# Context norms as late steps, the first norm's factor applied late, and shift columns made in the filler

## The chip, the cores and the metric

One core of one Trainium2 chip. TensorE (PE) multiplies matrices; its weight loads are listed as PEld. VectorE is DVE, ScalarE is ACT, GpSimd is POOL, and SyncE (SP) issues the transfers. The metric is the device time of one execution in microseconds (us).

## The reference

Two models, one after the other, on `x` of 512 tokens by 1024 features, all in float32.

The first has two layers. Each layer is: a gated feed-forward block (SwiGLU, inner width 2816), a mixer (sparse attention beside a gated MLP), and a second feed-forward block. Each of the three starts with an RMS norm whose scale and shift come from a vector `c` through a large matrix (`ada_w`): `n = rms(h) * g * (1 + scale) + shift`. The first model ends with `rms(h) * final_g`.

The second model has two layers on `x` (512 tokens) and on a context `ctx` (256 tokens). Layer 0 mixes tokens by mean pooling over windows of 2, 4, 8 and 16 positions, one window size for each quarter of the features, and then by a 256x256 matrix for each quarter; layer 1 by attention. After each mixer comes an MLP with squared ReLU (inner width 4096). All norms are modulated in the same way. Layer 0 runs on the context too, and layer 1 reads its result:

```
y = pool_mixer(modulate(rms_norm(x, g_mix_pre), sh1, sc1))
x = x + gt1 * rms_norm(y, g_mix_post)
m = sq_relu_mlp(modulate(rms_norm(x, g_mlp_pre), sh2, sc2))
x = x + gt2 * rms_norm(m, g_mlp_post)
```

## The kernel before

**Layout and products.** The residual `h` is kept transposed, features on partitions, as eight chunks of 128x512. Every float32 factor is split into a rounded part and a remainder (`hi`, `lo`), and a product is three matmuls (`mm3`, lines 114 to 116). A weight tile is loaded to one of three `raw` buffers (`wload`), copied to `whi` by ACT (line 98), and its remainder `wlo` is made by DVE or POOL (line 100). `psum()` takes one of six banks `mm`; two more banks, `aux`, take small products.

**Order of the queues.** The program is written as Python that traces instructions. A planner then orders each engine's queue: trace order is the priority, and its own estimates of durations decide what it takes to be ready. Where an instruction's input is later than estimated, the engine stands before it.

**Norms.** `Rms.add` squares a chunk on ACT and adds it into `ssum` on DVE or POOL (line 150). `mean` multiplies `ssum` by ones on PE (line 163), `rsqrt` takes eleven small DVE instructions (lines 128 to 133), `bcast` spreads the factor over the partitions by four PE transposes (line 202). `RmsPE` (line 181 and 183) multiplies each squared chunk by ones on PE instead and sums in PSUM; it is used once, for the pooled `y`.

**First tiles of a block.** `Pre` lets PE start on a block's first four weight tiles before the norm is known. The tail of the block before calls `Pre.chunk` for each new chunk of `h`; `Pre.issue` then multiplies the weights by the unnormalised chunks and applies the factor afterwards (`take`, line 377). The part of the product that comes from the shift is one column for each tile: `Pre.shift` multiplies the raw tile by the shift on POOL and sums it (lines 269, 274, 276), `column` finishes it by a product with ones (line 288), `bias` copies the four columns to `shb` (line 341). All this lies in the block's beginning, where DVE and PE also work on the norm.

**Filler.** Each feed-forward block (`ffn`) runs side work between its products: `run_steps(filler, nf[0])` after each pair of input tiles and `nf[1]` after each two output tiles. It consists of the products with `ada_w` (`ada_steps`, line 399, tiles `adaw` in three buffers), and in the last block, `ffn(1, 1)`, also of `ctx_steps`: the context's norm, `pool_mix`, the norm of its result, the residual and the next norm. In `pool_mix` each quarter `g` does two chunks of pooling on DVE and ACT and then at once its two products; the three norms are each one step.

**The pool stage.** The tail of `ffn(1, 1)` is `FinalTail`: it keeps two sums of squares, and multiplies each chunk by the pooling matrices (`project`). Four tables (`band`) are loaded and copied by ACT at line 1183 before the last output tiles start. After the block comes the pool stage of `x`, with steps of the context's MLP (`ctx`, `mlp_steps`) put between by hand (`WEAVE`): first factors (`factors`, line 1218), rescaled tiles (`pooled`, line 1234), then for each of eight chunks a product with the band (`windows`, lines 1247 and 1251), a copy (1366), the corrected edges (1369), the sum of squares, and line 1371, which applies the first model's last norm to `h`. Then `ry.finish()`, the residual (`post`, lines 1077 and 1078) with `Pre.chunk`, the first MLP tiles (`issue_two`), and the normed chunks (`normed`, lines 218 and 224). The context's MLP has, for each of eight parts, four input steps of 24 matmuls and eight output steps of 12, all 256 wide.

Of the kernel before, what the change touches and what calls it, by code (L numbers as in the profile page):

```python
# [18 lines left out]
D = 1024  # L19
# [18 lines left out]
WEAVE = (1, 3, 4, 1.65, 1)  # L38
# [13 lines left out]
def build(tc, d, stop=99):  # L52
# [83 lines left out]
    class Rms:  # L136


        def __init__(self, N, tmp, tag=""):
            self.N, self.n, self.tmp = N, 0, tmp  # L140
            p = norm_p if N == S and not tag else cur["cx"]
            self.acc = p.tile([128, N], F32, name=f"ssum{N}{tag}", tag=f"ssum{N}{tag}")
# [16 lines left out]
        def mean_steps(self):  # L159
            nt = self.N // 128  # L160
            st = psum(aux, "aux")
            for j in range(nt):
                T.matmul(st[:, j:j + 1], self.acc[:, j * 128:(j + 1) * 128], ones[:, 0:1], start=True, stop=True)
                yield
            v = small.tile([128, nt], F32, name="rs_v", tag="rs_v")
            V.tensor_scalar(v, st[:, :nt], 1.0 / D, EPS, op0=OP.mult, op1=OP.add)
            yield v
# [3 lines left out]

    class RmsPE(Rms):


        def __init__(self, N, tmp):
            self.N, self.n, self.tmp = N, 0, tmp
            self.st = psum(aux, "aux")

        def add(self, src, scale=1.0, eng=None):
            sq = self.tmp("sq")[:, :self.N]  # L180
            A.activation(sq, src, AF.Square, scale=scale)
            for j in range(self.N // 128):
                T.matmul(self.st[:, j:j + 1], sq[:, j * 128:(j + 1) * 128], ones[:, 0:1],
                         start=self.n + j == 0, stop=self.n == DC - 1 and j == self.N // 128 - 1)
            self.n += 1

        def mean_steps(self):
            nt = self.N // 128
            v = small.tile([128, nt], F32, name="rs_v", tag="rs_v")
            V.tensor_scalar(v, self.st[:, :nt], 1.0 / D, EPS, op0=OP.mult, op1=OP.add)  # L190
            yield v
# [34 lines left out]

    class Pre:
# [3 lines left out]
        def __init__(self, gs, sh, tmp):  # L231
            self.gs, self.sh, self.tmp = gs, sh, tmp
            self.rms = Rms(S, tmp)
            self.hi, self.lo = [], []
            self.cols = psum(aux, "aux")
            self.pss = []
            self.scaled = {}

        def chunk(self, k, src):
            hi, lo = rtile(), rtile()  # L240
            A.activation(hi, src, AF.Copy, scale=self.gs[:, k:k + 1])  # L241
            V.scalar_tensor_tensor(lo, src, self.gs[:, k:k + 1], hi.bitcast(F32), op0=OP.mult, op1=OP.subtract)
            self.hi.append(hi)
            self.lo.append(lo)
            self.rms.add(src, eng=G if k < 4 else V)
# [17 lines left out]
        def shift(self, raw):  # L263

            u = [shp_p.tile([128, 256], F32, name="shp", tag="shp") for _ in range(2)]
            n = 2
            for e, k in enumerate((0, 2, 4, 6)):
                o = u[min(e, 1)]
                G.tensor_tensor(o.rearrange("p (k m) -> p k m", k=n),  # L269
                                raw[:, k * 128:(k + n) * 128].rearrange("p (k m) -> p k m", k=n),  # L270
                                self.sh[:, k:k + n].rearrange("p (k o) -> p k o", o=1).to_broadcast([128, n, 128]),
                                op=OP.mult)
                if e > 0:
                    G.tensor_tensor(u[0], u[0], o, op=OP.add)  # L274
            r = shp_p.tile([128, 128], F32, name="shu", tag="shu", bufs=3)
            G.tensor_tensor(r, u[0][:, :128], u[0][:, 128:256], op=OP.add)
            return r

        def issue_two(self, srcs):

            self.issue(srcs, two=True)

        def issue(self, srcs, pss=(None,) * 4, two=False):
# [8 lines left out]
            def get(n):  # L292
                raw = srcs[n]()
                parts.append(wsplit(raw))
                us.append(self.shift(raw))
                self.pss.append(pss[n] if pss[n] is not None else psum())
# [27 lines left out]
            for i in range(4):  # L324
                column(i)
            self.bias(4)
# [217 lines left out]
    def pre_tail(mods, g, jsh=0, jsc=1):  # L544

        box = []

        def make(tmp):
            box.append(Pre(*modcols(mods, g, jsh, jsc), tmp))
            return box[0].chunk  # L550

        return box, make
# [468 lines left out]

    def norm_g(l, s):
        return pc("norm_g", (l * 3 + s) * 8)
# [3 lines left out]
    for l in range(L):  # L1027
        modsA, modsB = (mods_tile("m1", 24), mods_tile("m2", 24)) if l == 0 else (m1, m2)
        box, tail = pre_tail(modsA, norm_g(l, 1))
        if l == 0:  # L1030
            fill = lambda p, ph: chain(ada1(p, 0, 1, modsA), ada1(p, 0, 2, modsB))
            ffn(l, 0, mods0, fill, None, tail, (2, 2), start)
        else:
            ml = [mods_tile("ml", 48), mods_tile("mcx", 48)]
            ffn(l, 0, mods0, lambda p, ph: ada2(p, 0, ml), pre, tail, (2, 2))
# [47 lines left out]
    def pool_mix(x, N, bc, gs, sh, ph, inv, wp, parts, ytile, used=None):  # L1083
# [5 lines left out]

        wide = ph.wide  # L1090

        for g in range(4):
            w = WINDOWS[g]
            dhi, dlo = parts(g)
            for kk in range(2):
# [3 lines left out]
                if used is not None:  # L1099
                    used(k)  # L1100
# [16 lines left out]
                split(dhi(kk), dlo(kk), df)  # L1117
                yield
            whi, wlo = wget(wp[:, g * 512:(g + 1) * 512], 512)
            for m2 in range(2):  # L1120
                m = 2 * g + m2
                ps = psum()[:, :N]
                dense(ps, whi[:, m2 * 256:], wlo[:, m2 * 256:], 2, dhi, dlo)
                A.activation(ytile(m), ps, AF.Copy, scale=ps_scale[:, m:m + 1])
                rms_y.add(ytile(m))
                yield
        yield rms_y

    def ctx_steps(ph):

        SY.dma_start(cx, d["ctxT"])
        rc = Rms(C, ph.tmp)
        for k in range(DC):
            rc.add(cx[:, k])
            yield
        gs, sh = modcols(mcx, pc("g_mix_pre_2"), 0, 1)
        bc = rc.finish()
        bcs = cx_p.tile([128, C], F32, name="bcc", tag="bcc")
        A.activation(bcs, bc, AF.Copy)
# [16 lines left out]
        bc = ry.finish()  # L1156
        bcs = cx_p.tile([128, C], F32, name="bcc", tag="bcc")
        A.activation(bcs, bc, AF.Copy)
        post(cx, lambda k: ys[k // 2][:, k % 2], bcs, col, C, ph.tmp, lambda k, x: rc.add(x))
        yield  # L1160
        bc = rc.finish()
        bcs = cx_p.tile([128, C], F32, name="bcc", tag="bcc")
        A.activation(bcs, bc, AF.Copy)
# [7 lines left out]
    class FinalTail:  # L1171
# [4 lines left out]
        def __call__(self, tmp):  # L1176
            self.a, self.b = Rms(S, tmp), Rms(S, tmp, "b")
            gs, _ = modcols(ml, pc("g_mix_pre_2"), 0, 1)
            self.gf = colprod(gs, pc("final_g"))
# [7 lines left out]
        def chunk(self, k, src):  # L1187
            if k in (2, 4, 6):
                self.project(k // 2 - 1)
            self.a.add(src, eng=G if k < 7 else V)  # L1190
            self.b.add(src, pc("final_g")[:, k:k + 1], eng=G if k < 7 else V)
            hi, lo = rtile(), rtile()
            A.activation(hi, src, AF.Copy, scale=self.gf[:, k:k + 1])
            V.scalar_tensor_tensor(lo, src, self.gf[:, k:k + 1], hi.bitcast(F32), op0=OP.mult, op1=OP.subtract)
            self.u.append((hi, lo))

# [16 lines left out]
        def factors(self):  # L1213
# [11 lines left out]
            return r[:, 0:4], r[:, 4:8]  # L1225
# [28 lines left out]

    ft = FinalTail()
    ffn(1, 1, modsB, lambda p, ph: chain(ada2(p, 1, [ml1, mc1]), ctx_steps(ph)), pre, ft, (3, 3))
# [45 lines left out]
    with ExitStack() as st:  # L1302
# [57 lines left out]
        zs = []  # L1360
        for m in range(DC):
            if m in (0, 2):
                zs.append(ft.pooled(r12, m // 2))
# [11 lines left out]
        box, tail = pre_tail(ml, pc("g_mlp_pre_2"), 3, 4)  # L1375
        weave(post_steps(h, lambda k: yl[:, k], bcl, col, S, tmp, tail(tmp)), 0)
        pre = box[0]
        pre.issue_two([(lambda q=q: wload(d["mlp_in"][0, q // 2, :, (q % 2) * 1024:(q % 2) * 1024 + 1024])) for q in range(4)])
        run_steps(ctx, WEAVE[4])
        ph.n_tiles()  # L1380
        pre.normed(ph.nhi, ph.nlo)
        if stop <= 7:
            st.close()
            nst.close()
            return finish_debug()
# [393 lines left out]
```

## Time and profile before

| | us |
|---|---|
| three runs | 3662.05 (median), 3661.65, 3667.33 |
| the profiled execution | 3667.38 |
| its span, first to last instruction | 3665.6 |
| PE busy | 3493.1 (95%) |
| DVE busy | 2311.3 (63%) |
| ACT busy | 1461.0 (40%) |
| POOL busy | 484.2 (13%) |

The granted clock of PE is 0.975 of 2.4 GHz on average. A share of busy time is an average over stages; a busy PE can be one at half its clock.

### The profile page before, as it was taken

To read this page: it belongs to the slowest core of one execution; us is meant where nothing else is said; L and a number is where in the kernel's file an instruction comes from. 1 tells how busy PE (TensorE), PEld (TensorE's weight loads), DVE (VectorE), ACT (ScalarE), POOL (GpSimd) and SP (SyncE) were. 2 spreads that over 40 slices of the span, in tenths; PEclk is the share of its full clock that TensorE was granted. 3 is DMA by queue.
4 is the path that set the end of the run, shared out by engine and by line. 5 is a ranking of instruction groups with operands and counts; after the bars stand their busy time and mean duration, and the time that the engine had idled before them with its cause. 6 is when DMAs were issued, how large, how long until landed. Compare 5 with 4: busy or idle time off the path is not lost.

```text
span 3665.6 us, 44657 instructions
## 1 busy us (share of the span) xinstructions
PE 3493.1 (95%) x16980; PEld 2875.9 (78%) x16980; DVE 2311.3 (63%) x3696; ACT 1461.0 (40%) x2479; POOL 484.2 (13%) x471
## 2 busy tenths in 40 slices
PE   7999999999999999999999998989999988989998
PEld 5788877787878888887787877778888878767886
DVE  8863777458754995488647955665455588655434
ACT  3222475333223322366634223544333435644322
POOL 4000422030002100242004000240000021130000
PEclk9999999999999999999999999979999999999998
DMA  6862221236852573231134842314344421013232
GB/s 238 278 212 94 92 80 46 75 117 242 295 185 89 187 238 121 91 103 50 49 99 151 283 142 81 101 41 133 121 135 124 138 71 53 6 41 104 93 97 69
DMA packets 139256, 455.25 MB, mean 124 GB/s; under 512 B 16676, under 2 KB 19104, under 8 KB 138912
## 3 DMA queue, kind: packets, MB, share of 16 engines
q1 hardware_dynamic: 139040, 452.39, 37.6%
q8 instruction: 133, 2.18, 0.2%
q14 instruction: 83, 0.68, 0.1%
HBM read 450.23 MB, written 2.10 MB: 123 GB/s over the span
## 4 chain that ended last, share of the span: by engine, by line
PE 46%; DVE 6%; ACT 2%; POOL 2%; issue 1%; DMA 0%; DVEq 0%; ACTq 0%; POOLq 0%
PE mm L114 13%; PE mm L116 13%; PE mm L115 12%; DVE wlo L100 1%; POOL shp L269 1%; PE aux L1597 1%; PE aux L862 0%; DVE nt L218 0%; PE o L830 0%; POOL shp L274 0%; DVE h L1078 0%; ACT whi L98 0%; PE o L115 0%; PE o L831 0%; PE o L114 0%
## 5 line engine op out<-in xcount | busy, mean ns | idle before, releaser
L98 ACT ACTIVATE whi<-raw 128x1024 fp32r<-128x1024 f32 (+2 forms) x636 | 620.5, 977 | 1478.0 <-PE mm L115 1068.5
L100 DVE TENSOR_TENSOR wlo<-raw,whi 128x1024 fp32r<-128x1024 f32 (+3 forms) x607 | 697.8, 1152 | 516.5 <-ACT whi L98 508.3
L114 PE MATMUL mm<-n,whi 128*128 128x512 f32 x2096 | 832.2, 397 | 13.8 <-DVE px L377 9.5
L116 PE MATMUL mm<-n,wlo 128*128 128x512 f32 x2096 | 825.8, 395 | 2.7 <-DVE wlo L100 2.5
L115 PE MATMUL mm<-n,whi 128*128 128x512 f32 x2096 | 823.9, 393 | 0.4 <-DVE n L224 0.3
L114 PEld LDWEIGHTS mm<-n,whi 128*128 128x128 f32 x2096 | 396.8, 189 | 98.1 <-issue 11.1
L116 PEld LDWEIGHTS mm<-n,wlo 128*128 128x128 f32 x2096 | 396.1, 189 | 93.4 <-DVE wlo L100 5.2
L115 PEld LDWEIGHTS mm<-n,whi 128*128 128x128 f32 x2096 | 396.6, 189 | 85.4 <-POOL n L108 1.1
L399 DVE SCALAR_TENSOR_TENSOR junk<-adaw,crow 128x1024 f32<-128x1024 f32 x288 | 353.5, 1227 | 74.8 <-DMA adaw<-adaT 53.0
L114 PE MATMUL mm<-r,whi 128*128 128x512 f32 x960 | 381.2, 397 | 7.4 <-ACT whi L98 6.1
L116 PE MATMUL mm<-r,wlo 128*128 128x512 f32 x960 | 379.6, 395 | 0.0
L115 PE MATMUL mm<-r,whi 128*128 128x512 f32 x960 | 376.6, 392 | 0.8 <-DVE r L108 0.8
L114 PEld LDWEIGHTS mm<-r,whi 128*128 128x128 f32 x960 | 181.4, 189 | 46.7 <-ACT whi L98 6.6
L150 POOL TENSOR_TENSOR ssum<-ssum,sq 128x512 f32<-128x512 f32 x30 | 44.9, 1497 | 1291.9 <-ACT sq L149 1291.7
L116 PEld LDWEIGHTS mm<-r,wlo 128*128 128x128 f32 x960 | 181.2, 189 | 42.3 <-issue 0.5
L115 PEld LDWEIGHTS mm<-r,whi 128*128 128x128 f32 x960 | 181.5, 189 | 41.8 <-DVE r L108 1.4
L114 PE MATMUL mm<-hid,whi 128*128 128x512 f32 x448 | 177.1, 395 | 0.0
L116 PE MATMUL mm<-hid,wlo 128*128 128x512 f32 x448 | 176.1, 393 | 0.0
L115 PE MATMUL mm<-hid,whi 128*128 128x512 f32 x448 | 175.1, 391 | 0.0
L539 DVE SCALAR_TENSOR_TENSOR h<-mm,hg,h 128x512 f32<-128x512 f32 x96 | 71.9, 749 | 135.1 <-PE mm L116 135.1
L301 PE MATMUL mm<-r,whi 128*128 128x512 f32 x384 | 128.8, 411 | 18.0 <-ACT r L241 16.6
L521 DVE TENSOR_TENSOR hd<-mm,sil 128x512 f32<-128x512 f32 x79 | 54.4, 689 | 111.7 <-PE mm L116 111.5
(494 smaller groups left out, 5831.8 us busy)
## 6 DMA issues: line engine op xcount, KB each, us to landing
adaw<-adaT SPq DMA_DIRECT2D x240, 512.0 KB, 4.8
raw<-ffn_in SPq DMA_DIRECT2D x170, 512.0 KB, 4.6
raw<-mlp_in SPq DMA_DIRECT2D x96, 512.0 KB, 3.8
raw<-ffn_out SPq DMA_DIRECT2D x64, 512.0 KB, 3.9
raw<-mlp_out SPq DMA_DIRECT2D x64, 512.0 KB, 3.7
raw<-mlp_out SPq DMA_DIRECT2D x64, 256.0 KB, 2.9
raw<-ffn_out SPq DMA_DIRECT2D x32, 384.0 KB, 3.1
raw<-mix_zb SPq DMA_DIRECT2D x16, 512.0 KB, 3.6
```

The lines of the kernel that those rows point to most:

```text
L98: A.activation(hi[:, :F], raw, AF.Copy)
L100: (eng or cur["lo"]).tensor_tensor(lo[:, :F], raw, hi[:, :F], op=OP.subtract)
L114: T.matmul(ps, lh, rh, start=start, stop=False)
L115: T.matmul(ps, lh, rl, start=False, stop=False)
L116: T.matmul(ps, ll, rh, start=False, stop=stop)
L150: self.last = (eng or V).tensor_tensor(self.acc, self.acc, sq, op=OP.add)
L269: G.tensor_tensor(o.rearrange("p (k m) -> p k m", k=n), raw[:, k * 128:(k + n) * 128].rearrange("p (k m) -> p k m", k=n), self.sh[:, k:k + ...
L301: T.matmul(self.pss[n], w[:, sl], x, start=k + e == 0, stop=k == DC - 1 and e == 2)
L399: V.scalar_tensor_tensor(junk, w, 1.0, cs[v], op0=OP.mult, op1=OP.mult, accum_out=mods[v][:, j * 8 + m:j * 8 + m + 1])
L521: V.tensor_tensor(hd, pss[1], sil, op=OP.mult)
L539: V.scalar_tensor_tensor(h[:, m], ps, hg[:, m:m + 1], h[:, m], op0=OP.mult, op1=OP.add)
L1597: T.transpose(pt[:, q * 128:(q + 1) * 128], P[q][:, j * 128:(j + 1) * 128], ident)
```

## The change

1. Shift columns. `shift_steps`, new, makes the four columns of a block's first tiles inside a filler: it loads the raw tile a second time into an `adaw` buffer, runs the products on POOL, and in its next step the column on PE and a DVE copy. This is done for both mixers and for the MLP after the pool stage (twelve tiles); `Pre` then gets the finished columns and `issue` makes none. The fillers' rates become (3, 2) in `ffn(0, 0)` and (2, 3) in `ffn(1, 0)`.
2. Context. Each norm of `ctx_steps` becomes three steps (`row`); the two products of a quarter are traced after the pooling of the next quarter's chunks.
3. `FinalTail`. `h` is multiplied by `final_g` in place, chunk by chunk, and each band table is loaded at its chunk.
4. The factor of the first model's last norm, `r1`, is not applied in the pool loop. The pool's residual is formed for `h / r1` (its factor is multiplied by `s1 = v * r1`, the next norm's epsilon by `v`), and `h` is multiplied by `r1` after `normed`.
5. Pool stage. `RmsPE` becomes `Rms`; three context steps run inside the loop, at chunk 4; the first two MLP tiles are multiplied chunk by chunk as the residual is formed (`both`), the other two afterwards (`last_two`). `slow` puts all sums of squares there on DVE.

```diff
-WEAVE = (1, 3, 4, 1.65, 1)
+WEAVE = (2, 3, 3, 1.65, 3)
+    def shift_steps(p, sh, srcs, b):
+        for i, src in enumerate(srcs):
+            w = p.tile([128, 1024], F32, name="adaw", tag="adaw", bufs=3)
+            SY.dma_start(w, src)
+            r = shift_products(sh, w)
+            yield
+            c = psum(aux, "aux")
+            T.matmul(c[:, 0:1], r, ones[:, 0:1], start=True, stop=True)
+            V.tensor_copy(b[:, i:i + 1], c[:, 0:1])
+            yield
...
+        def first_two(self, srcs):
+            self.parts = [wsplit(src()) for src in srcs]
+            self.pss += [psum() for _ in srcs]
+        def both(self, k):
+            sl = slice(k * 128, (k + 1) * 128)
+            for ps, (wh, wl) in zip(self.pss, self.parts):
+                mm3(ps, wh[:, sl], wl[:, sl], self.hi[k], self.lo[k], k == 0, k == DC - 1)
+        def last_two(self, srcs):
+            steps = chain(self.rstd(0), self.rstd(1))
...
-            ffn(l, 0, mods0, fill, None, tail, (2, 2), start)
+            ffn(l, 0, mods0, fill, None, tail, (3, 2), start)
...
+        def project(g, dhi, dlo):
...
                 split(dhi(kk), dlo(kk), df)
+                next(late, None)
                 yield
-            whi, wlo = wget(wp[:, g * 512:(g + 1) * 512], 512)
...
+            run_steps(late)
+            late = project(g, dhi, dlo)
...
+        def row(rms, box):
+            v = rms.mean()
+            yield
+            r = rsqrt(v, 2)
+            yield
+            t = cx_p.tile([128, C], F32, name="bcc", tag="bcc")
+            A.activation(t, bcast(r, C), AF.Copy)
+            box.append(t)
+            yield
...
-            for g in range(4):
-                A.activation(self.band[:, g], wload(d["band"][:, g], S + 2 * BAND), AF.Copy)
...
-            self.b.add(src, pc("final_g")[:, k:k + 1], eng=G if k < 7 else V)
+            A.activation(src, src, AF.Copy, scale=pc("final_g")[:, k:k + 1])
...
+            self.b.add(src, eng=G if not last else V)
+            if k < 4:
+                A.activation(self.band[:, k], wload(d["band"][:, k], S + 2 * BAND), AF.Copy)
...
-        r1, r12 = ft.factors()
+        r1, r12, va = ft.factors()
+        V.tensor_scalar(eps, va, EPS, None, op0=OP.mult)
+        V.tensor_tensor(s1, va, r1, op=OP.mult)
         run_steps(ctx, WEAVE[1])
-        b1 = bcast(r1, S)
-        b1s = ph.hid_p.tile([128, S], F32, name="b1s", tag="hid0")
-        A.activation(b1s, b1, AF.Copy)
-        ry = RmsPE(S, tmp)
+        ry = Rms(S, tmp)
...
-            V.scalar_tensor_tensor(h[:, m], h[:, m], pc("final_g")[:, m:m + 1], b1s, op0=OP.mult, op1=OP.mult)
+            if m == 4:
+                run_steps(ctx, WEAVE[2])
+        v = ry.mean()
         col = colprod(ml[:, 16:24], pc("g_mix_post_2"))
-        run_steps(ctx, WEAVE[2])
-        bcl = ry.finish()
...
+        pre = Pre(*modcols(ml, pc("g_mlp_pre_2"), 3, 4), tmp, mlp_cols, eps, True)
+        pre.first_two([lambda q=q: wload(mlp_src(0, q)) for q in range(2)])
+        r = rsqrt(v, 4)
+        V.tensor_tensor(r, r, s1, op=OP.mult)
+        bcl = bcast(r, S)
+        post(h, lambda k: yl[:, k], bcl, col, S, tmp, chunk)
+        pre.last_two([lambda q=q: wload(mlp_src(0, q)) for q in range(2, 4)])
         run_steps(ctx, WEAVE[4])
         ph.n_tiles()
         pre.normed(ph.nhi, ph.nlo)
+        for k in range(DC):
+            V.tensor_tensor(h[:, k], h[:, k], b1s, op=OP.mult)
```

## Rows read from the trace of the kernel before

**Rows 1.** The page, span and PE busy.

```profile
span 3665.6 us, 44657 instructions
PE 3493.1 (95%) x16980; PEld 2875.9 (78%) x16980; DVE 2311.3 (63%) x3696; ACT 1461.0 (40%) x2479; POOL 484.2 (13%) x471
```

**Rows 2.** Stretches: length, busy PE PEld DVE ACT POOL, PE clock, DMA share, GB/s.

```profile
440.00:455.00 15.00, 12.95 (x74) 12.47 (x73) 13.23 (x16) 10.26 (x15) 8.60 (x8) 0.77 0.25 90
...
2195.00:2210.00 15.00, 7.75 (x29) 6.19 (x28) 7.69 (x26) 3.58 (x7) 0.14 (x2) 0.66 0.11 30
2265.00:2280.00 15.00, 9.14 (x32) 7.17 (x31) 9.31 (x23) 4.21 (x8) 0.14 (x2) 0.77 0.28 93
2320.00:2335.00 15.00, 8.87 (x31) 6.56 (x30) 5.87 (x8) 7.30 (x10) 0.00 (x0) 0.77 0.56 175
2335.00:2371.00 36.00, 36.00 (x194) 31.26 (x193) 18.89 (x23) 22.75 (x36) 20.51 (x13) 1.00 0.33 99
2376.00:2401.00 25.00, 17.84 (x122) 17.28 (x120) 19.22 (x37) 12.34 (x24) 10.65 (x7) 0.85 0.24 66
2401.00:2435.00 34.00, 33.48 (x147) 32.17 (x148) 10.77 (x26) 11.79 (x19) 13.67 (x17) 0.50 0.09 30
2435.00:2470.00 35.00, 23.81 (x99) 16.06 (x98) 29.41 (x45) 14.83 (x23) 19.75 (x19) 0.95 0.16 45
```

**Rows 3.** Timeline of PE, matmuls before which PE stood (idle us, releaser).

```profile
411.42 0.70 PE L301 MATMUL s<-r,whi 128*128 128x512 f32 x2 [1.48 <-DVE h L539]
443.81 2.88 PE L737 MATMUL aux<-B,raw 128*128 128x62 f32 x16 [2.05 <-POOL B L701]
...
1588.87 2.00 PE L737 MATMUL aux<-B,raw 128*128 128x62 f32 x16 [2.06 <-POOL B L701]
...
2200.38 0.66 PE L202 MATMUL aux<-ident,rs_y 128*128 128x128 f32 x2 [3.98 <-DVE rs_y L133]
2204.31 0.58 PE L114 MATMUL mm<-nc,whi 128*128 128x256 f32 x1 [3.27 <-ACT nc L107]
...
2272.02 0.58 PE L114 MATMUL mm<-nc,whi 128*128 128x256 f32 x1 [5.86 <-ACT nc L107]
...
2327.99 0.80 PE L114 MATMUL mm<-r,whi 128*128 128x512 f32 x1 [6.13 <-ACT whi L98]
...
2379.04 0.39 PE L1208 MATMUL mm<-whi,r 128*128 128x256 f32 x1 [2.85 <-DVE r L1194]
...
2401.49 1.87 PE L183 MATMUL aux<-ones,sq 128*128 128x1 f32 x8 [4.81 <-ACT sq L181]
...
2440.60 0.96 PE L301 MATMUL mm<-r,whi 128*128 128x512 f32 x3 [3.67 <-ACT r L241]
```

**Rows 4.** Groups by line, 2376 to 2437: count, busy us, mean ns, idle before.

```profile
L183 PE MATMUL aux<-ones,sq 128*128 128x1 f32 x64 | 14.7, 351 | 4.8 <-ACT sq L181 4.8
...
L1366 ACT ACTIVATE yl<-mm,par 128x512 f32<-128x512 f32 x8 | 5.5, 683 | 13.8 <-PE mm L1251 13.8
...
L181 ACT ACTIVATE sq<-yl 128x512 f32<-128x512 f32 x8 | 5.1, 632 | 5.4 <-DVE yl L1369 5.4
```

**Rows 5.** Timeline of PE: one `mean` product at the full clock.

```profile
2462.97 0.95 PE L163 MATMUL aux<-ones,ssum 128*128 128x1 f32 x8
```

**Rows 6.** Groups of DVE by line, 394 to 426, then 2437 to 2498.

```profile
L150 DVE TENSOR_TENSOR ssum<-ssum,sq 128x512 f32<-128x512 f32 x4 | 4.5, 1128 | 0.0
...
L150 DVE TENSOR_TENSOR ssum<-ssum,sq 128x512 f32<-128x512 f32 x4 | 2.7, 686 | 1.2 <-POOL ssum L150 1.2
```

**Rows 7.** Groups of POOL by line, 390 to 430; then what line 288 waited for.

```profile
L269 POOL TENSOR_TENSOR shp<-raw,m 128x256 f32<-128x256 f32 x16 | 13.5, 855 | 2.7 <-DMA raw<-mix_ck 2.1
L274 POOL TENSOR_TENSOR shp<-shp 128x256 f32<-128x256 f32 x12 | 11.1, 925 | 0.9
...
  POOL shu L276: 11.8, 10
```

**Rows 8.** The page, transfers: KB each, us from issue to landing.

```profile
adaw<-adaT SPq DMA_DIRECT2D x240, 512.0 KB, 4.8
```

More of the change, by code (lines that the diff above doesn't have):

```diff
@@ L170, in finish @@
             return bcast(rsqrt(self.mean(), self.N // 128), self.N)
[L172 to L191, printed above, removed]
     def bcast(r, N):
@@ L244, in chunk @@
             self.lo.append(lo)
-            self.rms.add(src, eng=G if k < 4 else V)
+            self.rms.add(src, eng=G if k < 4 and not self.slow else V)
         def rstd(self, part):
@@ L263, in shift @@
         def shift(self, raw):
[L265 to L281, printed above, removed]
+            return shift_products(self.sh, raw)
+        def first_two(self, srcs):
[7 more added lines that the diff above has]
+            steps = chain(self.rstd(0), self.rstd(1))
+            for n, src in enumerate(srcs):
+                parts = wsplit(src())
+                self.pss.append(psum())
+                for k in range(DC):
+                    sl = slice(k * 128, (k + 1) * 128)
+                    for e, (w, x) in enumerate(((parts[0], self.hi[k]), (parts[0], self.lo[k]), (parts[1], self.hi[k]))):
+                        T.matmul(self.pss[2 + n], w[:, sl], x, start=k + e == 0, stop=k == DC - 1 and e == 2)
+                        if n == 1 or k > 1:
+                            if not (n == 0 and k > 4) and not (n == 1 and k < 2):
+                                next(steps, None)
+            run_steps(steps)
         def issue(self, srcs, pss=(None,) * 4, two=False):
@@ L294, in get @@
                 parts.append(wsplit(raw))
-                us.append(self.shift(raw))
+                if self.cols is not None:
+                    us.append(self.shift(raw))
                 self.pss.append(pss[n] if pss[n] is not None else psum())
@@ L323, in issue @@
                 part(3, k)
-            for i in range(4):
-                column(i)
-            self.bias(4)
+            if self.cols is not None:
+                for i in range(4):
+                    column(i)
+                self.bias(4)
         def product(self, ps, parts, n):
@@ L1090, in pool_mix @@
         wide = ph.wide
+        def project(g, dhi, dlo):
+            whi, wlo = wget(wp[:, g * 512:(g + 1) * 512], 512)
+            for m2 in range(2):
+                m = 2 * g + m2
+                ps = psum()[:, :N]
+                dense(ps, whi[:, m2 * 256:], wlo[:, m2 * 256:], 2, dhi, dlo)
+                A.activation(ytile(m), ps, AF.Copy, scale=ps_scale[:, m:m + 1])
+                rms_y.add(ytile(m))
+                yield
+        late = iter(())
         for g in range(4):
@@ L1117, in pool_mix @@
                 split(dhi(kk), dlo(kk), df)
+                next(late, None)
                 yield
-            whi, wlo = wget(wp[:, g * 512:(g + 1) * 512], 512)
[L1120 to L1126, printed above, removed]
+            run_steps(late)
+            late = project(g, dhi, dlo)
+        for _ in late:
+            yield
         yield rms_y
@@ L1155, in ctx_steps @@
         gs, sh = modcols(mcx, pc("g_mlp_pre_2"), 3, 4)
[L1156 to L1163, printed above, removed]
+        yield from row(ry, box)
+        bcs = box.pop()
+        for k, _ in enumerate(post_steps(cx, lambda k: ys[k // 2][:, k % 2], bcs, col, C, ph.tmp, lambda k, x: rc.add(x))):
+            if k % 4 == 3:
+                yield
+        yield from row(rc, box)
+        bcs = box.pop()
         n = [[nctile() for _ in range(4)] for _ in range(2)]
@@ L1224, in factors @@
             r = rsqrt(v, 8)
[L1225 removed]
+            return r[:, 0:4], r[:, 4:8], v[:, 0:4]
         def pooled(self, r12, half_):
```

99 lines of the change are left out of this document (67 added, 32 removed).

## Prediction

> **What bounds the kernel now.** I read the page first. PE is busy 95% of the span [rows 1], so time can only come from three things: PE idle time, PE busy at half its clock, and PE work taken out. I then looked at stretches of 10 us over the whole span and kept those that the change touches [rows 2], and for these the instructions before which PE stood [rows 3]. In a stretch row the reader should compare the PE busy time with the length, and then look at the granted clock: 0.50 is 1.2 GHz and 1.00 is 2.4 GHz, so the time spent at the low level is twice (1 - clock) times the length, and half of what PE does in it is lost.
>
> Four places matter. (A) The start of the two mixers: PE stands 1.48 us before the first tiles, 2.05 and 2.06 us before the products with `B`, and in the first mixer the clock then falls [rows 2, 3]. (B) The context steps in the last feed-forward block: 3.98, 3.27 and 5.86 us [rows 3], each time with a clock that falls in the wait and comes back some 6 us after it, in the stretches from 2195 and 2265 [rows 2]. (C) The band tables: 6.13 us before the last output tiles [rows 2, 3]. (D) The pool stage of `x`, from 2376: waits of 2.85, 4.81 and 3.67 us [rows 3], and 34 us in which PE is 98% busy at the clock 0.50, from 2401 [rows 2]. From 2435 DVE sets the pace: 29.4 of 35 us against 23.8 on PE [rows 2].
>
> **A, the shift columns.** Removed from each mixer's start: four POOL products of some 6.6 us each, ((13.5 + 11.1) us of lines 269 and 274, and a short sum, over four tiles) [rows 7], four columns and the `bias` copy. While POOL does them, a DVE add takes 1128 ns instead of 686 [rows 6]; some ten DVE operations ahead of the first tiles are stretched so, 0.4 us each, which covers the wait of 1.48. The waits of 2.05 and 2.06 end with a chain norm, `U`, `B`; it loses the stretching of `rsqrt` and of the normed chunks (2 us) and DVE's wait for the last column. PE comes to it earlier too, so I count three quarters of the idle time, 5.6 of which 4.2. At the low clock the first mixer spends 2 x 0.23 x 15 = 6.9 us; half is lost, 3.4; I take half of that, as a shorter wait need not drop the clock: 1.7. Sum A: 6 us, bounds 0 and 9.
>
> The columns themselves cost PE the same in the filler. What is added there: twelve loads of 512 KB, 4.8 us to land [rows 8], twelve POOL products, twelve columns, twelve DVE copies. SP's queue: a load now waits for a buffer that a 6.6 us product holds, and the next weight tile is queued behind it. Three raw buffers cover that, as a tile keeps PE busy for 24 matmuls; without the cover it is up to 6.6 us for each of three phases, in which a fourth load meets three buffers. On DVE the weight remainders are queued behind the copy, and on PE all matmuls behind the column. A step lies between product and column, and the other columns give the price of a misjudged order: in the whole kernel line 288 and its weight loads waited 11.8 us in ten cases for 28 columns [rows 7], 0.4 each, 5 us for twelve. I take 1 us, with the faster rates (3, 2) and (2, 3) at nothing, since the filler's side work runs ahead of its place already; bounds 0 and 5.
>
> The products also slow DVE in the fillers. By rows 6 the factor is 1.64, on 12 x 6.6 = 79 us of POOL time, so up to 31 us more DVE time. I cost it at nothing, as PE sets the pace there and DVE has time left (7.7 busy of 15 from 2195, 9.3 of 15 from 2265) [rows 2]; without that cover the 31 us are a rival, below. The Trainium skill, GPSIMD Engine Reference, section Specifications, says that POOL's SBUF interfaces are shared with VectorE and that instructions with two SBUF inputs contend. The trace agrees: 1128 against 686 ns. By that rule the contention is moved, not removed, and the sum would be 31 us smaller where DVE is the pace.
>
> **B, the context's steps.** The waits sum to 13.1 us. At the low clock the two stretches spend 10.2 and 6.9 us [rows 2]; without the idle parts (3.27 after a fall, and some 1.5) 6 and 5.3 are left, half of it lost: 5.7. So 18.8 us are there. With the products one quarter late, inputs of three of the four quarters still come from the same group of three steps, but only one chunk's chain is left before them instead of two or the norm's as well. The norm's three parts stand at 53, 54 and 55 of the filler's steps, with no product of the block between the sum and the spreading, so the wait of 3.98 may stay. I take 11; bounds 0 and 18.8.
>
> **C, the band.** 6.13 idle, and 4.3 us of work at the low clock (6.9 us by [rows 2], less the end of the wait), half lost: 8.3. Added on ACT from 2335: eight scalings of `h` at 683 ns, the price of line 1366, also a scaled copy of 128x512 [rows 4], and four band copies of 800 columns, 1.07 us by the same rate: 9.7 on 22.75 of 36 us [rows 2]. That fits, but barely in the first chunks, which hold the bands. I take 1.8 us off: 6.5; bounds 3 and 8.3.
>
> **D, the pool stage.** (1) One more context step of 24 matmuls before `project(3)` takes about 2.8 us and covers the wait of 2.85; with it goes the low clock until 2387, 2 x 0.15 x 25 = 7.5 us, half lost: 3.7. A new wait for the first rescaled tiles takes 1.5. Sum 5. (2) `RmsPE` is 14.7 us on PE [rows 4]; `Rms` needs one `mean`, 0.95 [rows 5]: 13.7. PE stood 4.81 before its first product, behind line 1371 on DVE: 4.8. (3) The other 34 - 14.7 = 19.3 us from 2401 run at the low level; at the full one they take 9.6 less. (4) Against that: ACT needs a copy and a square for each chunk, 1.3 us by eight [rows 4], the second set of rescaled tiles and three context steps, some 14.7 us, where PE needs 12.4: 2.3. After the last chunk the chain copy, edges, square, add, mean, `rsqrt`, spreading, residual is bare, about 6.5 us of PE idle time where 3.67 stood [rows 3]: 2.9. So 5 + 13.7 + 4.8 + 9.6 - 5.2 = 27.9. (5) The residual: on DVE a chunk is four operations of about 0.69; without POOL's products beside them and with its adds, some 2.7 us less than before. Then eight products with `b1s`, 0.69 each [rows 6], 5.5 us, are new on DVE; two more context steps with their remainders on POOL cover part. I count this at nothing, bounds -5 and 5.
>
> Whether the clock is back in the loop is the open point. The row shows PE nearly always busy and still at 1.2 GHz from 2401 to 2435; it fell in the wait of 4.81 and rose only after context products. I take half of the 9.6: D is 23; bounds 10 and 33. The Trainium skill, TensorE: Matmul & The Clock Gate, section Terms, says that a monitor watches how busy PE is and gates its clock. By busy time as the profile counts it the clock should have risen in that stretch, and D would be 28; the row differs, and the measurement decides.
>
> **Sum.** 6 - 1 + 11 + 6.5 + 23 = 45.5, less 1 us for the start of the kernel, where transfers are dense: 44.5. The profiled execution took 3667.4 us, span 3665.6 and 1.8 around it; it would become 3623. The median of the runs is 5.3 us lower, so 3618.
>
> **The rivals.** (i) The loop stays at 1.2 GHz: nothing of the 9.6, and not the 3.7. D is 14.6, less 2 for the bare chain at this level, so 10.4 below the forecast's 23; the time is 3628. For it: the 34 us row. Against: the one-column products go. (ii) The context's waits only change their place, since the planner's estimate stays short: B is 0, the time 3629. For it: the sum and the spreading still adjacent. (iii) The moved products slow DVE where it is the pace: 31 us of the 44.5, 3649. Against: DVE time left in rows 2. (iv) The other side: PE stands in front of each new column, because the planner doesn't see POOL's real pace, as the two waits for `B` (2.05 and 2.06, [rows 3]) show. A whole product exposed is 12 x 6.6 = 79 us, giving 3697. It is slower by 0.2% (7.3 us, about what a measurement of this kernel tells from no change) from 4.3 us for each column. Against: 0.4 us by rows 7. (v) The planner gives the steps their old places in the queues and the bare chain takes D's gain: within 7 us of before.
>
> **How the numbers follow.** The forecast has 0.55, (i) 0.13, (ii) 0.12, (iii) 0.07, (iv) 0.06, (v) 0.07. The range goes from 3598, most of the upper bounds together, to 3648, (i) and (ii) together with half of (iii). Faster by over 0.2%: the first four, 0.87; within: 0.07; slower: 0.06.
>
> **What the profile of the changed kernel would show.** A: no line 269 products in the mixers' starts, and waits for `B` under 1 us. B: no wait over 2 us before `nc` products. C: no wait before the last output tiles, ACT below its limit. D: the loop takes 17 to 20 us at the clock 1.00, the residual starts some 22 us sooner counted from `project(3)`, and DVE stays the pace behind it. Wrong would make it: waits before the columns, a loop at 0.50, or a DVE queue that is late for the first MLP products.

## The result, and the profile after

The changed kernel takes 3627.5 us (median of 4 runs, 3625.5 to 3629.5) against 3664.0 for the kernel before beside it: ratio 0.990, 95% interval 0.9883 to 0.9917. It is faster by 36.5 us where 44.5 were forecast; 3627.5 lies in the range given. In a second measurement it took 3630.0 against 3664.3 (0.9903, 0.9889 to 0.9918). The profiled execution has a span of 3627.7, so 37.9 less than [rows 1]. Its page, span and PE:

```profile
span 3627.7 us, 44600 instructions
PE 3472.6 (96%) x16924; PEld 2861.7 (79%) x16924; DVE 2299.2 (63%) x3715; ACT 1462.9 (40%) x2487; POOL 476.0 (13%) x470
```

PE is 20.5 us less busy, and it stands 17.4 us less (155.1 against 172.5). To see where, I cut the span at instructions that both kernels have: the last addition to `h` of a block or a mixer, the last residual addition of the pool stage, the first residual addition behind the MLP. The lengths of these stages are the measure of this whole study. A run's median moves with everything in 3.6 ms, a stage only with what lies in it. "Low" is the time that PE's clock was at 1.2 GHz in the first mixer, summed as twice (1 - clock) times the length over stretches of 10 us.

| kernel (in the order of the experiments) | median us | ratio, interval | block (0,0) ends | mixer 0 (low) | block (1,1) | pool stage | MLP |
|---|---|---|---|---|---|---|---|
| before | 3664.0 | | 411.3 | 406.1 (14) | 413.7 | 88.1 | 534.9 |
| changed | 3627.5 | 0.9883-0.9917 | 412.4 | 407.2 (17) | 387.2 | 68.9 | 536.8 |
| changed, again | 3630.0 | 0.9889-0.9918 | 413.7 | 407.0 (21) | 389.4 | 69.9 | 538.0 |
| 1 mixers' columns back | 3622.7 | 0.9871-0.9901 | 410.7 | 405.3 (17) | 387.6 | 69.0 | 536.1 |
| 2 norms in single steps | 3640.8 | 0.9920-0.9946 | 413.4 | 404.3 (14) | 401.5 | 69.0 | 536.5 |
| 3 products not late | 3628.5 | 0.9892-0.9919 | 414.1 | 410.5 (24) | 387.0 | 69.0 | 536.0 |
| 4 bands at the start | 3632.9 | 0.9902-0.9932 | 413.5 | 404.8 (14) | 393.9 | 69.0 | 537.5 |
| 5 squares summed on PE | 3638.8 | 0.9920-0.9947 | 414.7 | 404.5 (17) | 385.6 | 83.3 | 536.1 |
| 6 first tiles behind | 3624.6 | 0.9863-0.9897 | 413.3 | 402.7 (10) | 385.7 | 68.5 | 538.1 |
| 7 `h` scaled late | 3622.8 | 0.9872-0.9901 | 413.8 | 404.7 (14) | 389.7 | 69.8 | 531.6 |
| 8 = 1 and 7 | 3618.5 | 0.9859-0.9897 | 410.6 | 411.0 (24) | 386.0 | 68.9 | 531.7 |
| 9 = 8, steps spread | 3613.9 | 0.9832-0.9866 | 410.7 | 404.7 (17) | 386.3 | 64.7 | 532.1 |
| 10 = 8, steps in the loop | 3619.0 | 0.9854-0.9893 | 410.4 | 402.2 (0) | 386.0 | 69.2 | 530.9 |
| 11 = 9, columns ahead, rate 2 | 3608.7 | 0.9835-0.9868 | 409.4 | 402.3 (10) | 389.3 | 64.6 | 532.3 |

So block (1,1) gave 26.5 us, the pool stage 19.2; block (0,0) lost, and the MLP lost about 2. What the mixers seem to lose (here 1.1 and 4.0) is not the change, as other executions with the same code show: the first mixer in the table's other rows, and the second, which takes 402.0 to 405.8 with the columns ahead and 401.5 to 405.6 without.

**A.** PE's timeline in the changed kernel: the waits that stood as 1.48, 2.05 and 2.06 in [rows 3].

```profile
412.50 0.70 PE L324 MATMUL s<-r,whi 128*128 128x512 f32 x2 [0.94 <-ACT whi L98]
...
443.93 2.45 PE L761 MATMUL aux<-B,raw 128*128 128x62 f32 x15 [2.24 <-POOL B L725]
...
1590.73 2.60 PE L761 MATMUL aux<-B,raw 128*128 128x62 f32 x16 [2.23 <-POOL B L725]
```

The first is a third shorter, and both waits for `B` are longer, not gone. The twelve columns themselves wait for nothing worth a row.

**B and C.** All that PE waited for between 2100 and the end of block (1,1), where [rows 3] had 3.98, 3.27, 5.86 and 6.13:

```profile
PE mm L114 <- ACT whi L98: 0.4, 1, 0.4
PE aux L163 <- DVE ssum L150: 0.2, 1, 0.2
```

**D.** The pool stage and the 39.4 us behind it in the changed kernel, and then the same stage before (columns as in [rows 2]).

```profile
2353.00:2421.90 68.90, 55.82 (x320) 50.27 (x319) 52.56 (x99) 38.62 (x66) 11.28 (x7) 0.80 0.21 62
2421.90:2461.30 39.40, 27.81 (x162) 24.11 (x161) 33.77 (x56) 19.92 (x33) 5.37 (x3) 0.83 0.30 90
```

```profile
2372.50:2460.60 88.10, 70.91 (x358) 63.07 (x356) 55.30 (x91) 38.80 (x67) 44.84 (x41) 0.75 0.14 42
```

PE works 15.1 us less here, and stands 13.1 instead of 17.2; by the clock it is low for 28 us (2 x 0.20 x 68.9) instead of 44. What it waits for now, from its timeline:

```profile
2370.66 0.38 PE L114 MATMUL mm<-hc,whi 128*128 128x256 f32 x1 [1.76 <-ACT hc L107]
2372.16 0.38 PE L115 MATMUL mm<-hc,whi 128*128 128x256 f32 x1 [1.11 <-DVE hc L108]
2374.26 0.58 PE L114 MATMUL mm<-hc,whi 128*128 128x256 f32 x1 [0.97 <-ACT hc L107]
2375.83 0.58 PE L115 MATMUL mm<-hc,whi 128*128 128x256 f32 x1 [0.86 <-DVE hc L108]
...
2396.91 1.36 PE L163 MATMUL aux<-ones,ssum 128*128 128x1 f32 x8 [3.77 <-DVE ssum L150]
...
2400.99 1.08 PE L184 MATMUL aux<-ident,rs_y 128*128 128x128 f32 x4 [1.76 <-DVE rs_y L1436]
2404.93 1.22 PE L114 MATMUL mm<-r,whi 128*128 128x512 f32 x2 [2.85 <-ACT r L254]
...
2449.81 0.55 PE L114 MATMUL mm<-nc,whi 128*128 128x256 f32 x1 [7.24 <-DVE px L401]
```

The first four are the fifth context step, whose operands are made by the four just before it. The next three are the bare chain behind the loop. The last is new, and DVE's timeline says why:

```profile
2441.52 1.40 DVE L200 SCALAR_TENSOR_TENSOR nt<-h,gs,bcs 128x512 f32<-128x512 f32 x2
2442.84 0.68 DVE L1449 TENSOR_TENSOR h<-h,b1s 128x512 f32<-128x512 f32 x1
2443.44 1.40 DVE L206 SCALAR_TENSOR_TENSOR n<-nt,ml,n 128x512 fp32r<-128x512 f32 x2
2444.77 4.29 DVE L1449 TENSOR_TENSOR h<-h,b1s 128x512 f32<-128x512 f32 x7
2448.98 0.68 DVE L401 TENSOR_TENSOR px<-mm,bcs 128x512 f32<-128x512 f32 x1
```

The eight products with `b1s` stand in front of the scaling that empties the first MLP tile, and PE's next product waits for it.

### The profile page after: what moved, and what is told of

The parts are those of the page before. It is cut to its first block, busy times and chain, and to the rows that moved or that the text cites. A ratio compares the mean times of both kernels' runs of the same rounds, so it can differ in the third digit from the quotient of the medians.

```text
span 3627.7 us, 44600 instructions
## 1 busy us (share of the span) xinstructions
PE 3472.6 (96%) x16924; PEld 2861.7 (79%) x16924; DVE 2299.2 (63%) x3715; ACT 1462.9 (40%) x2487; POOL 476.0 (13%) x470
## 4 chain that ended last, share of the span: by engine, by line
PE 63%; DVE 7%; ACT 2%; issue 1%; POOL 1%; DMA 1%; SPq 0%; DVEq 0%; ACTq 0%; POOLq 0%
PE mm L114 18%; PE mm L116 18%; PE mm L115 18%; DVE nt L200 1%; DVE wlo L100 1%; PE mm L324 1%; PE aux L1665 1%; PE aux L886 1%; DVE h L1108 0%; DVE n L206 0%; PE o L854 0%; ACT whi L98 0%; DVE ssum L150 0%; POOL shp L215 0%; PE o L115 0%
## 5 line engine op out<-in xcount | busy, mean ns | idle before, releaser
L114 PE MATMUL mm<-n,whi 128*128 128x512 f32 x2096 | 831.5, 397 | 14.2 <-ACT nt L202 9.2
L114 PE MATMUL mm<-r,whi 128*128 128x512 f32 x976 | 385.5, 396 | 4.6 <-ACT r L254 3.1
L115 PE MATMUL mm<-r,whi 128*128 128x512 f32 x976 | 382.3, 392 | 0.2 <-DVE r L108 0.2
L108 DVE TENSOR_TENSOR ptl<-aux,pth 128x512 fp32r<-128x512 f32 x144 | 94.7, 684 | 43.8 <-ACT pth L107 43.2
```

Of the source, the lines that this page charges most:

```text
L108: (eng or V).tensor_tensor(lo, src, hi, op=OP.subtract)
L114: T.matmul(ps, lh, rh, start=start, stop=False)
L115: T.matmul(ps, lh, rl, start=False, stop=False)
```

## The experiments

Each but the last three is the changed kernel with one part undone or moved.

**1. The mixers' columns back in the mixers**, with the old rates.

```diff
-        box, tail = pre_tail(modsA, norm_g(l, 1), cols=cols)
+        box, tail = pre_tail(modsA, norm_g(l, 1))
...
-            fill = lambda p, ph: chain(ada1(p, 0, 1, modsA), ada1(p, 0, 2, modsB), ahead(p))
-            ffn(l, 0, mods0, fill, None, tail, (3, 2), start)
+            fill = lambda p, ph: chain(ada1(p, 0, 1, modsA), ada1(p, 0, 2, modsB))
+            ffn(l, 0, mods0, fill, None, tail, (2, 2), start)
```

> The changed kernel with the mixers' shift columns put back to the mixers' starts (no column steps in the fillers of the first feed-forward block of a layer, rates (2, 2) again). Changed kernel: 3627.5. Theory 1, the forecast's A: the step is worth 6 - 1 us, so 3632 to 3633. Theory 2, from the landmarks of the two traces (the two mixers ended 1.1 and 3.9 us later counted from their start, the two blocks before them 1.1 and 0.5): A lost some 6 us, so 3621. Theory 3: the mixers' loss is only where the clock happened to fall in one profiled execution: within 2 us of 3627.5.

3622.7, so A's step gained nothing; theory 2 is nearest. By the ratio alone the two kernels are not told apart (0.9871 to 0.9901 against 0.9883 to 0.9917), so I go by the stages. The landmarks of theory 2 were half luck: the first mixer is 405.3 on average in the nine executions with the columns ahead (402.3 to 410.5) and 405.9 in the five without (402.2 to 411.0), the second 403.5 and 403.8. What does not vary is block (0,0): with the columns ahead and rate 3 it ends at 412.4 to 414.7 (eight executions, mean 413.6), without at 410.4 to 411.3 (five, mean 410.7). The loss is 2.9 us, and it lies there.

**2. The context's norms as single steps again, and its residual too**, and **3. its pool products beside their own quarter again**.

```diff
 (2)
-        yield from row(rc, box)
-        bcs = box.pop()
+        bc = rc.finish()
+        bcs = cx_p.tile([128, C], F32, name="bcc", tag="bcc")
+        A.activation(bcs, bc, AF.Copy)
...
 (3)
-                next(late, None)
                 yield
-            run_steps(late)
-            late = project(g, dhi, dlo)
+            whi, wlo = wget(wp[:, g * 512:(g + 1) * 512], 512)
...
```

> The changed kernel with only the context's norms (sum, factor, spreading) and residual put back into single steps, the pool products stay late. Theory 1, the forecast's B: the wait of 3.98 us stays in any case, so nothing is lost here: 3627 to 3629. Theory 2: the three separate steps took away the 3.98 us wait and its low clock, and part of the last: 3632 to 3637.

> The changed kernel with only the context's pool products put back beside their own quarter (norm's steps stay separate). Theory 1: the late products carry the two later waits, 3.27 and 5.86 us, and their low clock of about 5 us: 3638 to 3642. Theory 2: the norm's and the residual's separate steps carry most of B, and the late products little: 3628 to 3631.

Block (1,1) takes 387.3 on average in the ten executions that have all of B and C (385.6 to 389.7). With experiment 2 it takes 401.5, 14.2 more; the median of 3640.8 is above even theory 2's 3637. PE waits in it as before:

```profile
PE mm L114 <- ACT nc L107: 7.2, 2, 3.9
PE aux L184 <- DVE rs_y L133: 4.0, 1, 4.0
```

With the products beside their quarters it takes 387.0, and the waits are 1.2 and 0.2. That is theory 2 of experiment 3 (3628.5). So the separate steps carry B, though the run does not part the norms' links from the residual's steps; the late products alone add nothing to them. They shorten the third wait, from 5.86 to 3.9, where the norms are single. Both undone together was not run. Of the 26.4 us that the block gained on average, 14.2 are shown here and 6.6 by experiment 4; the other 5.6 no single run shows.

**4. The four bands copied before the first output tile again.**

```diff
+            for g in range(4):
+                A.activation(self.band[:, g], wload(d["band"][:, g], S + 2 * BAND), AF.Copy)
             self.u = []
...
-            if k < 4:
-                A.activation(self.band[:, k], wload(d["band"][:, k], S + 2 * BAND), AF.Copy)
```

> The changed kernel with the four band tables loaded and copied before the first output tile again. Theory 1, the forecast's C: the wait of 6.1 us and its low clock come back, less the smaller cover: 6.5 us more than the changed kernel on this chip. Theory 2: B's steps end sooner now and the planner puts the copies elsewhere, so the tables cost nothing: within 2 us.

Block (1,1) takes 393.9, 6.6 more, and the wait is back (of the 5.8, one is 5.5). By the stage that is theory 1. The median is only 2.9 above the changed kernel beside it (3632.9, runs from 3630.4 to 3641.5, against 3630.0), which does not decide between the theories.

```profile
PE mm L114 <- ACT whi L98: 5.8, 2, 5.5
```

**5. The loop's squares summed on PE again**, by the old class.

```diff
-        ry = Rms(S, tmp)
+        ry = RmsPE(S, tmp)
```

> The changed kernel with the squares of the pool loop summed on PE by one-column products again. Theory 1, the forecast's D (2) and (3): 13.7 us of PE work and part of the clock come back, 15 to 23 us more than the changed kernel. Theory 2: the sum on DVE and its bare chain (PE stands 3.77 us before the mean) cost part of that back, so 8 to 13 us more.

The pool stage takes 83.3 instead of 69.2 (mean of the eight that share its code): 14.1. The total is 8.8 above the changed kernel in that measurement, in theory 2's range; the stage lies just under theory 1's 15. The groups of PE in the stage, and the stage's row:

```profile
L186 PE MATMUL aux<-ones,sq 128*128 128x1 f32 x64 | 13.4, 330 | 3.2 <-ACT sq L184 3.2
```

```profile
2350.00:2433.30 83.30, 69.75 (x376) 63.52 (x375) 48.09 (x92) 38.93 (x66) 11.27 (x7) 0.73 0.18 51
```

PE works 13.9 us more than in the changed kernel, and its clock is low for 45 us (2 x 0.27 x 83.3), as in the kernel before (44), instead of 28. So what of the low clock went, went with the one-column products.

**6. The MLP's first two tiles issued behind the residual**, in the order of the other blocks.

```diff
-            pre.both(k)
...
-        pre.last_two([lambda q=q: wload(mlp_src(0, q)) for q in range(2, 4)])
+        pre.issue([(lambda q=q: wload(mlp_src(0, q))) for q in range(4)])
```

> The changed kernel, but with the MLP's first two tiles issued behind the residual in the order of the other blocks, not chunk by chunk within it (columns, late factor and the rest stay). Theory 1: the 16 chunks' products fill PE while DVE paces the residual, so without them 8 to 12 us more than the changed kernel (3627.5 and 3630.0 in two measurements). Theory 2: DVE's queue sets the end of the stage anyway (the hole of 7.24 us behind it shrinks by as much), so 0 to 4 us more.

Stage and MLP together 606.6 against 605.9 on average, which is theory 2's low end; the median, 3624.6, is not above the changed kernel's at all. So the order chunk by chunk gained nothing that shows. PE takes the tiles' products beside DVE in either order; the wait for `px` behind it is 4.14 instead of 7.24.

**7. `h` scaled late**: the eight products with `b1s` one per step from the MLP's fifth step on.

```diff
-        for k in range(DC):
-            V.tensor_tensor(h[:, k], h[:, k], b1s, op=OP.mult)
...
+        def scaled(p, gen):
+            for n, _ in enumerate(gen):
+                if p == 0 and 4 <= n < 12:
+                    V.tensor_tensor(h[:, n - 4], h[:, n - 4], b1s, op=OP.mult)
+                yield
```

> The changed kernel with the eight products of h with b1s one per step from the fifth step of the MLP on, instead of all before it (one more hidden pair in the shared tiles, as b1s keeps its buffer longer). Theory 1: they stand on DVE in front of the scalings that free the first tiles, and make 5 of the 7.24 us for which PE stands at 2442.6: 3622 to 3624. Theory 2: DVE is the pace of the whole start of the MLP, so they cost the same later: 3627 to 3628.

The MLP takes 531.7 on average in the five executions with this edit (530.9 to 532.3) and 536.9 in the eight with the products in front (536.0 to 538.1): 5.2, theory 1. In PE's timeline the wait is 1.07:

```profile
2444.55 0.55 PE L114 MATMUL mm<-nc,whi 128*128 128x256 f32 x1 [1.07 <-DVE px L401]
```

**8. Edits 1 and 7 together**, and the changed kernel again beside it.

> The changed kernel with the mixers' columns back in the mixers and the eight products of h with b1s one per step of the MLP: both edits that gained by themselves (4.8 and 4.7 us against the changed kernel's earlier median). Theory 1: they add up, 9 to 10 us less than the changed kernel. Theory 2: half of each was the difference between chips, 4 to 6 us less.

> The changed kernel once more, unedited, as the base for the other three on this chip and as a second profiled execution of it. Theory of the clock: the 17 us at the low level from 440 and the 17 us from 1585 in its first profile are a matter of the single execution, so this one shows other sums there (five kernels with this code had 10 to 24 and 0 to 17). Rival: they belong to this order of instructions, and come again within 2 us. Time 3625 to 3630.

11.5 us less than the changed kernel there, theory 1 and a little more. The stages explain 8.1 (2.9 + 5.2). The low clock in the mixers' starts did change between two executions of one kernel. These are the same stretch of the first mixer, 53 us behind its start, in the first execution and in the second:

```profile
465.50:479.20 13.70, 13.70 (x68) 13.47 (x68) 7.43 (x20) 5.33 (x12) 6.37 (x4) 0.50 0.51 161
```

```profile
466.80:480.50 13.70, 12.57 (x105) 11.63 (x103) 10.41 (x28) 8.07 (x23) 9.20 (x7) 1.00 0.53 172
```

The second execution has falls elsewhere that the first has not, so over a whole mixer the sums differ less: 17 and 21 us in the first mixer, 17 and 17 in the second. The places belong to the single execution; of the sums that is not shown.

**9 and 10. The context's MLP steps put elsewhere in the pool stage**, on top of 8. In 10 the two chain steps stand in the loop too.

```diff
-        run_steps(ctx, WEAVE[1])
+        run_steps(ctx, 2)
...
-                run_steps(ctx, WEAVE[2])
+                run_steps(ctx, 2)
+        run_steps(ctx, 1)
         v = ry.mean()
...
+        run_steps(ctx, 1)
         bcl = bcast(r, S)
```

> The kernel with both edits (mixers' columns back, h's products with b1s late) and the context's MLP steps in the pool stage put elsewhere: two instead of three before the loop, three in it instead of three, and one more between the residual's factor and its spreading. In the kernel with both edits alone (3618.5, ratio to before 0.9878) PE stands 1.76 + 1.12 + 0.97 + 0.87 us in front of the fifth step, 3.77 before the loop's sum and 1.77 before the spreading, and the clock is low for 37 us of the stage. Theory 1: the four waits of the fifth step go and the bare chain is covered, with some of the clock: 6 to 10 us less. Theory 2: the chain's instructions on ACT and DVE then wait behind those of the steps, so the waits only move: within 3 us.

> As the one before, but with all four steps after the fifth chunk of the loop and none between the factor and the spreading. Theory 1: only the waits in front of the fifth step go (4.7 us and a part of the low clock), the bare chain stays: 3 to 6 us less than the kernel with both edits alone (ratio to before 0.9878). Theory 2: that stretch is bound by the rescaled tiles, not by the step, so within 2 us.

With the steps spread the stage takes 64.7, 4.5 less than the average of 69.2, and the clock is 0.87 in it; that is between the two theories. Four steps in the loop give 69.2, nothing: the waits of the fifth step go, but PE then stands for the rescaled tiles and 5.33 instead of 3.77 before the sum. PE's waits in the stage sum to 13.4 us in number 8, 9.5 in number 9 and 13.3 in number 10. So the covered chain made the gain.

**11. Number 9 with the mixers' columns ahead, at the old rate.**

```diff
-            ffn(l, 0, mods0, fill, None, tail, (3, 2), start)
+            ffn(l, 0, mods0, fill, None, tail, (2, 2), start)
```

> The fastest kernel so far (3613.9, ratio to before 0.9849: late products of h, spread context steps, mixers' columns in the mixers), but with the mixers' columns made ahead as in the changed kernel and the first block's filler rate left at (2, 2) instead of (3, 2). In eight profiles with columns and rate 3 that block ended at 412.4 to 414.7, in the others at 410.4 to 411.3. Theory 1: the rate is what loses there, as a filler step on DVE comes between the start's own column sums: the block ends at 410.4 to 411.5, and the time is within 3 us of 3613.9, since the mixers' own durations did not differ (405.7 and 405.9 on average for the first). Theory 2: the columns themselves cost PE their 2 to 3 us in the filler: it ends at 413 or later, and the time is 3 to 6 us above.

Block (0,0) ends at 409.4, 1 us before theory 1's range: the rate loses there, not the columns. DVE's timelines at the start show how; the changed kernel, then number 1:

```profile
91.39 1.23 DVE L423 SCALAR_TENSOR_TENSOR junk<-adaw,crow 128x1024 f32<-128x1024 f32 x1 [1.07 <-DMA adaw<-adaT]
...
98.97 0.28 DVE L389 TENSOR_TENSOR raw<-raw 128x128 f32<-128x128 f32 x1
```

```profile
96.81 0.28 DVE L389 TENSOR_TENSOR raw<-raw 128x128 f32<-128x128 f32 x1
97.02 1.22 DVE L423 SCALAR_TENSOR_TENSOR junk<-adaw,crow 128x1024 f32<-128x1024 f32 x1
```

With rate 3 a filler product comes before the sums for the shift columns of the kernel's first tiles (line 389). The last of these starts 2.2 us later, and PE waits 2.8 us for them instead of 1.5. In all eight executions with rate 3 it starts at 98.97 to 100.44, in the six with rate 2 at 96.49 to 98.28. At 3608.7 this is the fastest kernel by its median; by the ratio it equals number 9.

## Why the prediction was right and wrong

The direction, the range and the three places of the gain were right. The sum was 8 us too large. By stages it is 41.3 where 44.5 was forecast: A and D were each 6 us too large, B 9 too small. That these errors nearly cancel is luck. The other 5 us are mostly what executions of one kernel differ by. The measured 3627.5 is nearer to the totals of rivals (i) and (ii), 3628 and 3629, than to the forecast's 3618; only the stages show that (ii) did not happen, and (i) only in part. The upper end of the range is added up wrongly: (i), (ii) and half of (iii) make 3655, not 3648. The result lies inside either.

**A: 6 - 1 - 1 forecast, about -2 measured** (0.9 in the two mixers, -2.9 in block (0,0)). Two steps failed. The first is the shorter wait for `B`: the chain to `B` was to lose the stretching of `rsqrt` and of the normed chunks. DVE's timeline of that chain before, then in the changed kernel:

```profile
419.52 0.16 DVE L166 TENSOR_SCALAR rs_v<-aux 128x4 f32<-128x4 f32 x1 [1.09 <-PE aux L163]
...
423.93 0.16 DVE L133 SCALAR_TENSOR_TENSOR rs_y<-rs_b,rs_y 128x4 f32<-128x4 f32 x1
424.04 2.88 DVE L100 TENSOR_TENSOR wlo<-raw,whi 128x1024 fp32r<-128x1024 f32 x2
426.88 2.08 DVE L218 SCALAR_TENSOR_TENSOR nt<-h,gs,bcs 128x512 f32<-128x512 f32 x3
...
436.38 0.16 DVE L341 COPY shb<-aux 128x4 f32<-128x4 f32 x1 [0.79 <-PE aux L288]
```

```profile
420.60 0.16 DVE L167 TENSOR_SCALAR rs_v<-aux 128x4 f32<-128x4 f32 x1 [2.81 <-PE aux L163]
...
422.79 0.16 DVE L133 SCALAR_TENSOR_TENSOR rs_y<-rs_b,rs_y 128x4 f32<-128x4 f32 x1
424.84 2.36 DVE L100 TENSOR_TENSOR wlo<-raw,whi 128x1024 fp32r<-128x1024 f32 x2 [1.89 <-ACT whi L98]
427.96 2.08 DVE L200 SCALAR_TENSOR_TENSOR nt<-h,gs,bcs 128x512 f32<-128x512 f32 x3 [0.76 <-ACT bcs L270]
```

`rsqrt` did get shorter, from 4.6 to 2.4 us. But DVE then stands 1.89 us for a weight copy and 0.76 for the spreading, and the first normed chunk starts 15.6 us after the block's end in both kernels. The normed chunks were never stretched: the products are over before them. This row of the kernel before was there to be read, POOL 0.00 while DVE is full:

```profile
425.00:435.00 10.00, 10.00 (x50) 8.28 (x48) 10.00 (x15) 5.80 (x9) 0.00 (x0) 1.00 0.29 96
```

What is left of the gain in the first mixer is DVE's wait and copy for the columns, 0.95 us; PE comes 1.15 us sooner, so its wait grows by 0.2.

The second step counted the faster rates at nothing, since the filler's side work runs ahead of its place. At the start of block (0,0) DVE sets the pace, and there a filler product stands in front of sums that PE waits for (experiment 11). The columns cost nothing that the stages show, so rival (iv), PE standing before each, did not come; nor did rival (iii). The contention is real [rows 6], but in blocks that PE paces the moved products slowed nothing (block (0,0) 409.4 with them, 410.7 without). The Trainium skill, GPSIMD Engine Reference, section Specifications, has the SBUF interfaces of POOL shared with VectorE, with contention where VectorE's instructions have two SBUF inputs; the trace agrees, 1128 ns for an add against 686 [rows 6].

**B: 11 forecast, about 20 measured** (26.4 in block (1,1), less 6.6 for C). "The wait of 3.98 may stay" failed: I took three neighbouring steps to mean no product of the block between the sum and the spreading. The planner put thirteen matmuls there, between the sum's product and the spreading's:

```profile
2194.08 0.58 PE L163 MATMUL aux<-ones,ssum 128*128 128x1 f32 x4 [0.21 <-DVE ssum L150]
...
2197.70 0.40 PE L184 MATMUL aux<-ident,rs_y 128*128 128x128 f32 x2
```

The upper bound of 18.8 was nearly the truth, and the part that I counted on, the late products, was not what carried it. Rival (ii) is refuted: no wait took their place.

**C: 6.5 forecast, 6.6 measured.** The net was right; its split into 8.3 and the ACT load no run shows.

**D: 23 forecast, 16.9 measured**: 14.1 for the sum on PE, 4.8 for the rest of the stage (88.1 - 83.3), which no run takes apart, and -2.0 in the MLP. Term (2), 18.5 less the bare chain's 2.9, is 15.6 against 14.1. Of (1), (3) and the 2.3 of (4), 7.5 together, 4.8 came: the added step covers the wait before `project(3)`, but with it the fifth step stands before the loop, and this one is late by 4.7 us, because it needs what the four before it make. The clock came back for part of the loop only, between the forecast's half and rival (i): from its first to its last product with the band the loop takes 20.7 us at the clock 0.67 (31.7 at 0.60 before), so 13.7 at the low level, where 17 to 20 us at 1.00 were to be seen. The residual starts 19 us sooner counted from `project(3)`, not 22. By the rule of the Trainium skill, TensorE: Matmul & The Clock Gate, section Terms, D would have been 28. The trace differs again: in this row of the changed kernel PE is busy all the time, and the clock is not at full speed.

```profile
2380.00:2390.00 10.00, 10.00 (x57) 9.81 (x57) 5.25 (x10) 7.00 (x11) 0.68 (x1) 0.64 0.18 54
```

Term (5), counted at nothing with a bound of -5, was -2.0: there the text named DVE as the pace, and did not ask what is queued behind the eight new products. What is queued are the scalings that free PSUM, and experiment 7 gives 5.2 for them.

The four terms make 41.3 by stages (-2.0, 26.4, 16.9). The profiled execution of the kernel before was 3.4 above the median beside it, so 37.9 by medians, against 36.5 measured; the 1.4 left are within the runs' spread.

## What to carry to other kernels

Cut a serial chain that is fed into other work (sum, factor, spreading) at each of its links: with the residual in steps too, that was worth 14 us here. Where DVE sets the pace, work with no due time belongs behind what frees a PSUM tile; eight small products in front of it cost 5.2 us. Compare stages, over several executions, before a few us are put down to an edit, and look in each stage for the engine that is full at that moment, not over the block.

## What the hardware showed beside that

The first mixer is the same code in the nine executions with the columns ahead, and its length goes with the clock: 402.3 and 402.7 us with 10 us at the low level, 404.3 to 404.8 with 14, 404.5 and 407.2 with 17, 407.0 with 21, 410.5 with 24. So the low time explains most of it, not all. Of those with the columns inside, the one with no time at the low level took 402.2, the one with 24 took 411.0. Block (0,1), which no edit touches, varies too, from 368.9 to 375.9, with the clock at full speed there but for 3 us in two of the executions, and with 1.2 to 7.0 us of PE idle time. A low stretch can be one in which PE is busy without a break, as the first of the two rows under experiment 8 shows, and the same stretch ran at full speed in the other execution. A wait of PE can so cost nothing or several us of low clock in the same order of instructions; what decides it is open.
